# A hybrid decoder trunk: normed input of three token chunks from x given with tokens as columns, instead of transpositions by TensorE

## The chip, the cores and the metric

The kernel runs on one core of one Trainium2 chip. Its time is the device time of one execution in microseconds (us), the median of several runs. TensorE multiplies and transposes (PE in the profile; its weight loads are PEld), VectorE (DVE) and GpSimd (POOL) do elementwise work, ScalarE (ACT) elementwise work and the copies out of PSUM; SyncE (SP) and ACT issue the transfers. Each engine takes its instructions in the order in which the program issued them.

## The reference

Sequence 2048, model width 1024, one layer, float32:

```python
h = x * rsqrt(mean(x * x, axis=-1) + EPS) * norm_g          # _rmsnorm
proj = h @ w_in + b_in                                      # 1024 -> 4096
ua, za, ub, zb, ga, gb = split(proj)                        # 512 512 512 512 1024 1024
ya = s5_branch(ua, ...) * silu(za)      # diagonal complex state-space layer, gelu, glu
yb = pool_branch(ub, ...) * silu(zb)    # means over windows of 2, 4, 8, 16 tokens
merged = sigmoid(ga) * (ya @ w_branch_a) + sigmoid(gb) * (yb @ w_branch_b)
return _rmsnorm(x + merged @ w_out, final_norm_g)
```

## The kernel before

All products are done in pairs of float32r: an operand is split into a high part, rounded on ACT, and a low part, the difference, taken on DVE or POOL; `mm3` then issues three matmuls (high by high, high by low, low by high) for each slice of 128 of the contraction. The result has output channels on the partitions and tokens along the free axis, so the normed input must be there with model channels on the partitions: the tile `hT[c]` holds it for token chunk c (four chunks of 512 tokens), as 8 slices k of 128 channels, high and low. A block (c, n) is one tile of 128 output channels by 512 tokens: 8 slices, 24 matmuls of 128x512.

The first stage does the four blocks n = 0 to 3 of `ua` for each chunk in turn, (0,0), (0,1), ... (3,3), and makes `hT` meanwhile, one chunk ahead. After a block ACT evicts it (`uo`) and issues its store (`Ud`). Chunk c + 1 is made so: four tiles `xt` of 128 tokens are loaded; `mean_square` sums their squares, and `rsqrt` makes the roots with ten operations of four columns on DVE; `norm_tiles` multiplies each tile by its roots, on ACT and DVE for chunk 1 and on POOL for chunks 2 and 3; after blocks (c, 2) and (c, 3) `transpose_tile` transposes four slices each on TensorE, 16 transpositions into PSUM (`psT`), and splits them on the way out, with the gain of the norm as scale (high on ACT, low on DVE). The blocks of the stages behind (`za`, then `ub`, `zb`, `ga`, `gb`, scan, branches, output) follow on TensorE without a pause that is planned.

Names of weights: `wt` are split weights for later blocks, `w_first` those of the first stage (n = 1 to 3), `raw` their two staging buffers; `pump` loads the next raw block and splits the one that is there, so a load waits on SP until a staging buffer is free. `Later` (`pv`) holds the small operations that make the state-space parameters (tiles of 128x32) and issues so many behind each block on DVE. `WARM` is 17 transpositions of the identity (`psw`) that run before there is data.

Of the kernel before, what the change touches and what calls it, by code (L numbers as in the profile page):

```python
# [21 lines left out]
T = 8  # L22
# [14 lines left out]
def hybrid_kernel(ctx: ExitStack, tc: tile.TileContext, x, norm_g, w_in, b_in, log_dt, lam_re, lam_im,  # L37
                  b_re, b_im, c_re, c_im, ssm_d, w_glu, b_glu, pool_w, pool_scale, w_a, w_b, w_out,
                  final_g, out):
# [129 lines left out]
    def w_in_job(n, target):  # L169
        def load(raw):  # L170
            SP.dma_start(out=raw.rearrange("p (k n) -> p k n", k=NK),
                         in_=w_in[0][:, n * 128:(n + 1) * 128].rearrange("(k p) n -> p k n", p=128))
        add_job(("in", n), load, target)

    def branch_job(c, n):
        def load(raw):
            r = raw.rearrange("p (b k n) -> p b k n", b=2, k=NB)
            for b, w in enumerate((w_a, w_b)):
                SP.dma_start(out=r[:, b], in_=w[0][:, n * 128:(n + 1) * 128].rearrange("(k p) n -> p k n", p=128))
        add_job(("br", c, n), load, plain)  # L180
# [120 lines left out]
    def load_params(d):  # L301
        ldt = d.tile([128, G], F32, name="ldt")
        SP.dma_start(out=ldt, in_=log_dt[0].partition_broadcast(128))
        lam = d1.tile([G, 2, 128], F32, name="lam")
        for i, src in enumerate((lam_re, lam_im)):
            for h in range(2):
                SP.dma_start(out=lam[:, i, h * 64:(h + 1) * 64], in_=src[0])
        dn = d1.tile([G, C], F32, name="dn")
        SP.dma_start(out=dn, in_=ssm_d[0].rearrange("(g c) -> g c", c=C))
        return ldt, lam, dn  # L310

    def params(d, V, ldt, lam, dn):
# [16 lines left out]
        psl = mstile("psl")  # L329
        for i in range(2):  # L330
            PE.transpose(psl[:, i * G:(i + 1) * G], lam[:, i, :], idn[0:G, 0:G])
        PE.transpose(psl[0:C, 2 * G:3 * G], dn, idn[0:G, 0:G])
        lr, li = small("lr"), small("li")
        V.tensor_copy(out=lr, in_=psl[:, 0:G])
        V.tensor_copy(out=li, in_=psl[:, G:2 * G])
        V.tensor_copy(out=dc, in_=psl[0:C, 2 * G:3 * G])
# [191 lines left out]
    xts = {}  # L528

    def load_x(c):  # L530

        for i in range(4):
            tt = 4 * c + i
            if c in (1, 2):
                xt = xp.tile([128, D], F32, tag="xt", bufs=8, name="xt")
            else:
                xt = d1.tile([128, D], F32, tag="xt", bufs=4, name="xt")
            k0 = (tt % 2) * 128
            SP.dma_start(out=xt, in_=xr[tt // 2, k0:k0 + 128, :])
            xts[tt] = xt  # L540

    def mean_square(c):

        ss = d1.tile([128, 4], F32, tag="ss", bufs=2, name="ss")
        v = d1.tile([128, 4], F32, tag="v", bufs=2, name="v")
        for i in range(4):
            if c == 1 and i > 1:
                V.scalar_tensor_tensor(out=hT[c][:, 1, i - 1:i + 1, :].rearrange("p k n -> p (k n)"),
                                       in0=xts[4 * c + i], scalar=1.0, in1=xts[4 * c + i], op0=ALU.mult,
                                       op1=ALU.mult, accum_out=ss[:, i:i + 1])  # L550
            else:
                k = 2 * i if c == 3 else 0
                A.activation(hT[c][:, 0, k:k + 2, :].rearrange("p k n -> p (k n)"), xts[4 * c + i], AF.Square,
                             accum_out=ss[:, i:i + 1])
        V.tensor_scalar(out=v, in0=ss, scalar1=1.0 / D, scalar2=EPS, op0=ALU.mult, op1=ALU.add)
        return rsqrt(d1, v, 4)

    def norm_tiles(c):
        rstd = mean_square(c)
        for i in range(4):  # L560
            xt = xts[4 * c + i]
            if c > 1:
                GP.tensor_tensor(out=xt, in0=xt, in1=rstd[:, i:i + 1].broadcast_to([128, D]), op=ALU.mult)
# [11 lines left out]
    def first_block():  # L575

        rstd = mean_square(0)
# [10 lines left out]
        load_x(2)  # L588
# [27 lines left out]
    rows = d1.tile([48, 128], F32, name="rows")  # L616
    A.dma_start(out=rows[0:32, :], in_=b_in[0].rearrange("(n p) -> n p", p=128))
    A.dma_start(out=rows[32:40, :], in_=norm_g[0].rearrange("(n p) -> n p", p=128))
    A.dma_start(out=rows[40:44, :], in_=b_glu[0].rearrange("(n p) -> n p", p=128))
    A.dma_start(out=rows[44:48, :], in_=pool_scale[0].rearrange("(n p) -> n p", p=128))  # L620
    make_identity(nc, idn)
    psr = mstile("psr")
    PE.transpose(psr[:, 0:48], rows, idn[0:48, 0:48])
    V.tensor_copy(out=cols, in_=psr[:, 0:48])
    V.tensor_scalar(out=half, in0=psr[:, 0:48], scalar1=0.5, scalar2=0.0, op0=ALU.mult, op1=ALU.add)
# [12 lines left out]
    load_x(1)  # L638
    pv = Later(V)
    for c in range(NCH):  # L640
        for n in range(NB):
# [25 lines left out]
            pv.issue(26 if c + 1 == NCH else 10 if n > 1 else 20)  # L667
# [502 lines left out]
    for c in range(NCH):  # L1170
# [83 lines left out]
```

## Time and profile before

| | before |
|---|---|
| time, median of 3 runs (lowest, highest) | 1194.56 us (1194.1, 1196.18) |
| the profiled execution's own time | 1194.22 us |
| its span, first to last instruction | 1192.4 us |
| mean granted TensorE clock | 0.998 of full speed |
| PE, DVE, ACT, POOL busy | 98%, 60%, 33%, 27% of the span |

Times in the views count from the start of the span. The 1.8 us between the span and the time lie around it. Matmuls overlap in the pipeline: one is shown with some 0.39 us, but the next starts 0.23 us later, so distances between starts are to be read. A granted clock of 1.00 is 2.4 GHz, 0.50 is 1.2 GHz.

### The profile page before, as it was taken

Reading aid. Unit: us, or ns where it says so; the run is one execution under the profiler, and the core shown is the slowest. Engines: PE = TensorE matmul, PEld = TensorE weight load, DVE = VectorE, ACT = ScalarE, POOL = GpSimd, SP = SyncE. Lnnn points to the kernel's source line nnn. Section 1 sums busy time; section 2 is a strip of 40 time slices with the busy share of each in tenths; the row PEclk is TensorE's granted clock in tenths of the full one; section 3 lists DMA queues with packets and bytes.
Section 4 is the critical chain, followed back from the end, with each engine's and each line's share of the span. In section 5 each row is a group of like instructions: output and inputs, shape, how many; then the busy total and the mean of one; then the engine's idle time right before and its main releaser. Section 6 shows DMA issues by size and latency. Waiting matters only on the chain. (4 is left out here: it accounts for less than half of the span.)

```text
span 1192.4 us, 14803 instructions
## 1 busy us (share of the span) xinstructions
PE 1172.4 (98%) x5413; PEld 971.4 (81%) x5413; DVE 709.9 (60%) x1320; ACT 396.5 (33%) x622; POOL 325.0 (27%) x223
## 2 busy tenths in 40 slices
PE   6999999999999999999999999999999999999997
PEld 5887877888888888888888888888878888888886
DVE  4588399164344664887778873047665755755614
ACT  6542222122222232444334442244333332323202
POOL 2321077011012122432234321234223313213313
PEclk9999999999999999999999999999999999999999
DMA  8412334202111332433334332287875563563602
GB/s 293 151 43 82 67 116 139 75 18 73 36 38 56 98 96 90 132 110 108 106 102 128 100 105 81 70 265 247 273 227 197 177 198 138 176 211 115 198 7 88
DMA packets 149783, 149.94 MB, mean 126 GB/s; under 512 B 23584, under 2 KB 111184, under 8 KB 149712
## 3 DMA queue, kind: packets, MB, share of 16 engines
q1 hardware_dynamic: 127568, 112.54, 31.1%
q10 hardware_dynamic: 22144, 36.47, 8.2%
q8 instruction: 42, 0.69, 0.2%
q14 instruction: 29, 0.24, 0.1%
HBM read 99.43 MB, written 49.55 MB: 125 GB/s over the span
## 5 line engine op out<-in xcount | busy, mean ns | idle before, releaser
L104 PE MATMUL mm<-hT,wt 128*128 128x512 f32 x960 | 375.6, 391 | 0.0
L105 PE MATMUL mm<-hT,wt 128*128 128x512 f32 x960 | 374.4, 390 | 0.7 <-DVE hT L100 0.7
L106 PE MATMUL mm<-hT,wt 128*128 128x512 f32 x960 | 374.0, 390 | 0.1
L105 PEld LDWEIGHTS mm<-hT,wt 128*128 128x128 f32 x960 | 180.3, 188 | 38.3 <-DVE hT L100 1.9
L106 PEld LDWEIGHTS mm<-hT,wt 128*128 128x128 f32 x960 | 180.2, 188 | 38.3 <-DVE wt L148 0.4
L104 PEld LDWEIGHTS mm<-hT,wt 128*128 128x128 f32 x960 | 180.3, 188 | 36.7
L98 POOL TENSOR_TENSOR wt<-raw,wt 128x1024 fp32r<-128x1024 f32 x29 | 83.3, 2874 | 321.6 <-ACT wt L96 321.6
L1046 ACT ACTIVATE go<-mm,half 128x512 f32<-128x512 f32 x64 | 44.0, 688 | 189.6 <-PE mm L106 184.5
L104 PE MATMUL mm<-yab,wt 128*128 128x512 f32 x256 | 99.8, 390 | 1.2 <-DVE gt L1186 1.1
L106 PE MATMUL mm<-yab,wt 128*128 128x512 f32 x256 | 99.6, 389 | 0.0
L105 PE MATMUL mm<-yab,wt 128*128 128x512 f32 x256 | 99.6, 389 | 0.0
L1188 POOL TENSOR_TENSOR m<-gt 128x512 f32<-128x512 f32 x32 | 51.5, 1611 | 136.2 <-DVE gt L1186 102.8
L96 ACT ACTIVATE wt<-raw 128x1024 fp32r<-128x1024 f32 x61 | 64.5, 1057 | 68.5 <-PE mm L106 41.6
L1143 POOL TENSOR_TENSOR xt<-r,gb 128x512 f32<-128x512 f32 (+1 forms) x33 | 41.0, 1258 | 126.3 <-DVE r L1141 123.9
L98 DVE TENSOR_TENSOR wt<-raw,wt 128x1024 fp32r<-128x1024 f32 x32 | 59.9, 1873 | 18.9 <-ACT wt L96 18.9
L857 ACT ACTIVATE st<-mm,half 128x512 f32<-128x512 f32 x32 | 22.0, 688 | 131.2 <-PE mm L106 98.5
L1186 DVE SCALAR_TENSOR_TENSOR gt<-gt,mm 128x512 f32<-128x512 f32 x64 | 42.8, 681 | 36.8 <-PE mm L106 32.1
L104 PEld LDWEIGHTS mm<-yab,wt 128*128 128x128 f32 x256 | 48.1, 188 | 11.9 <-issue 1.9
L106 PEld LDWEIGHTS mm<-yab,wt 128*128 128x128 f32 x256 | 48.0, 188 | 10.0
L105 PEld LDWEIGHTS mm<-yab,wt 128*128 128x128 f32 x256 | 48.1, 188 | 9.8
L105 PE MATMUL mm<-wo,mt 128*128 128x512 f32 (+1 forms) x136 | 51.2, 377 | 0.0
L104 PE MATMUL mm<-wo,mt 128*128 128x512 f32 (+1 forms) x136 | 51.2, 377 | 0.0
(274 smaller groups left out, 1872.2 us busy)
## 6 DMA issues: line engine op xcount, KB each, us to landing
xt<-in_x SPq DMA_DIRECT2D x32, 512.0 KB, 5.5
raw<-in_w_in SPq DMA_DIRECT2D x32, 512.0 KB, 4.3
Gd<-go ACTq DMA_DIRECT2D x64, 256.0 KB, 2.2
gt<-Gd SPq DMA_DIRECT2D x32, 512.0 KB, 4.9
raw<-in_w_branch_a SPq DMA_DIRECT2D x32, 256.0 KB, 2.8
raw<-in_w_branch_b SPq DMA_DIRECT2D x32, 256.0 KB, 3.2
out<-xt ACTq DMA_DIRECT2D x31, 256.0 KB, 2.3
Ud<-uo ACTq DMA_DIRECT2D x16, 256.0 KB, 2.5
```

The source lines that it names most:

```text
L96: A.activation(hi, src, AF.Copy, scale=1.0 if scale is None else scale)
L98: (eng or V).tensor_tensor(out=lo, in0=src, in1=hi.bitcast(F32), op=ALU.subtract)
L104: PE.matmul(ps, lhsT=sh, rhs=mh, start=first, stop=False)
L105: PE.matmul(ps, lhsT=sh, rhs=ml, start=False, stop=False)
L106: PE.matmul(ps, lhsT=sl, rhs=mh, start=False, stop=last)
L857: A.activation(t, ps, AF.Tanh, bias=hcol(n), scale=0.5)
L1046: A.activation(o, ps, AF.Tanh, bias=hcol(n), scale=0.5)
L1143: GP.tensor_tensor(out=xt, in0=r, in1=gb[:, cs], op=ALU.mult)
L1186: V.scalar_tensor_tensor(out=gt[:, b], in0=gt[:, b], scalar=1.0, in1=pss[b], op0=ALU.add, op1=ALU.mult)
L1188: GP.tensor_tensor(out=m, in0=gt[:, 0], in1=gt[:, 1], op=ALU.add)
```

## The change

Chunk 0 stays as it was. For chunks 1 to 3:

- A second copy of x, `x_t`, with tokens as columns, is given beside x (laid out on the host). `load_xT` loads four tiles `xT` of 128x2x512 per chunk, which have model channels on the partitions already.
- The rows of x are loaded once more, into two buffers `xrow`, for the sums of squares alone, all on ACT (`squares`, in two pairs); the roots are made as before (`root`).
- `norm_row` makes the row of roots: four matmuls with the roots, broadcast, as stationary operand and the identity as moving one give a tile `psR` in which each partition holds the roots of the 512 tokens; ACT copies it to `R`.
- `norm_tile` multiplies a slice by its gain and by `R` in one DVE operation in place, then splits it from SBUF: high on ACT, low on DVE.
- The 96 transpositions of these chunks, the multiplications by roots on ACT, DVE and POOL, and the squares on DVE are gone.
- Vectors and matrices that were transposed on the chip at the start (`rows`, `lam`, `dn`) come laid out; the blocks of `w_in`, `w_branch_a`, `w_branch_b` and `w_glu` come each in one piece, so that a partition's row is one run of 4 KB where it was eight of 512 B.
- The small operations of `Later` go 12 behind each block where it was 20 or 10 (26 in chunk 3 as before).

The diff, cut to what the text speaks of:

```diff
--- before.py
+++ after.py
...
     def w_in_job(n, target):
         def load(raw):
-            SP.dma_start(out=raw.rearrange("p (k n) -> p k n", k=NK),
-                         in_=w_in[0][:, n * 128:(n + 1) * 128].rearrange("(k p) n -> p k n", p=128))
+            SP.dma_start(out=raw, in_=w_in[n])
         add_job(("in", n), load, target)
...
     def load_params(d):
         ldt = d.tile([128, G], F32, name="ldt")
         SP.dma_start(out=ldt, in_=log_dt[0].partition_broadcast(128))
-        lam = d1.tile([G, 2, 128], F32, name="lam")
-        for i, src in enumerate((lam_re, lam_im)):
-            for h in range(2):
-                SP.dma_start(out=lam[:, i, h * 64:(h + 1) * 64], in_=src[0])
-        dn = d1.tile([G, C], F32, name="dn")
-        SP.dma_start(out=dn, in_=ssm_d[0].rearrange("(g c) -> g c", c=C))
-        return ldt, lam, dn
-
-    def params(d, V, ldt, lam, dn):
+        lr, li = (d.tile([128, G], F32, name=n) for n in ("lr", "li"))
+        SP.dma_start(out=lr, in_=lam_re)
+        SP.dma_start(out=li, in_=lam_im)
+        SP.dma_start(out=dc, in_=ssm_d)
+        return ldt, lr, li
+
+    def params(d, V, ldt, lr, li):
...
-        psl = mstile("psl")
-        for i in range(2):
-            PE.transpose(psl[:, i * G:(i + 1) * G], lam[:, i, :], idn[0:G, 0:G])
-        PE.transpose(psl[0:C, 2 * G:3 * G], dn, idn[0:G, 0:G])
-        lr, li = small("lr"), small("li")
-        V.tensor_copy(out=lr, in_=psl[:, 0:G])
-        V.tensor_copy(out=li, in_=psl[:, G:2 * G])
-        V.tensor_copy(out=dc, in_=psl[0:C, 2 * G:3 * G])
...
-    xts = {}
+    xts, xrows, roots = {}, {}, {}

     def load_x(c):

         for i in range(4):
+            xts[i] = xt = d1.tile([128, D], F32, tag="xt", bufs=4, name="xt")
+            k0 = (i % 2) * 128
+            SP.dma_start(out=xt, in_=xr[i // 2, k0:k0 + 128, :])
+
+    def load_xT(c):
+
+        for h in range(4):
+            if c in (1, 2):
+                t = xp.tile([128, 2, 512], F32, tag="xt", bufs=8, name="xT")
+            else:
+                t = d1.tile([128, 2, 512], F32, tag="xt", bufs=4, name="xT")
+            SP.dma_start(out=t, in_=x_t[256 * h:256 * h + 256, 512 * c:512 * c + 512].rearrange("(k p) n -> p k n", p=128))
+            xts[c, h] = t
+
+    def load_rows(c, tiles):
+
+        for i in tiles:
             tt = 4 * c + i
-            if c in (1, 2):
-                xt = xp.tile([128, D], F32, tag="xt", bufs=8, name="xt")
-            else:
-                xt = d1.tile([128, D], F32, tag="xt", bufs=4, name="xt")
             k0 = (tt % 2) * 128
-            SP.dma_start(out=xt, in_=xr[tt // 2, k0:k0 + 128, :])
-            xts[tt] = xt
-
-    def mean_square(c):
-
-        ss = d1.tile([128, 4], F32, tag="ss", bufs=2, name="ss")
+            xrows[c, i] = t = d1.tile([128, D], F32, tag="xrow", bufs=2, name="xrow")
+            SP.dma_start(out=t, in_=xr[tt // 2, k0:k0 + 128, :])
+
+    def root(c, ss):
         v = d1.tile([128, 4], F32, tag="v", bufs=2, name="v")
-        for i in range(4):
-            if c == 1 and i > 1:
-                V.scalar_tensor_tensor(out=hT[c][:, 1, i - 1:i + 1, :].rearrange("p k n -> p (k n)"),
-                                       in0=xts[4 * c + i], scalar=1.0, in1=xts[4 * c + i], op0=ALU.mult,
-                                       op1=ALU.mult, accum_out=ss[:, i:i + 1])
-            else:
-                k = 2 * i if c == 3 else 0
-                A.activation(hT[c][:, 0, k:k + 2, :].rearrange("p k n -> p (k n)"), xts[4 * c + i], AF.Square,
-                             accum_out=ss[:, i:i + 1])
         V.tensor_scalar(out=v, in0=ss, scalar1=1.0 / D, scalar2=EPS, op0=ALU.mult, op1=ALU.add)
         return rsqrt(d1, v, 4)

-    def norm_tiles(c):
-        rstd = mean_square(c)
+    sums1 = {}
+
+    def squares(c, tiles):
+        if c not in sums1:
+            sums1[c] = d1.tile([128, 4], F32, tag="ss", bufs=2, name="ss")
+        for i in tiles:
+            t = xrows.pop((c, i))
+            A.activation(t, t, AF.Square, accum_out=sums1[c][:, i:i + 1])
+        if 3 in tiles:
+            roots[c] = root(c, sums1.pop(c))
+
+    def norm_row(c):
+
+        rstd = roots[c]
+        ps = mstile("psR")
         for i in range(4):
-            xt = xts[4 * c + i]
-            if c > 1:
-                GP.tensor_tensor(out=xt, in0=xt, in1=rstd[:, i:i + 1].broadcast_to([128, D]), op=ALU.mult)
-            elif i % 2:
-                A.activation(xt, xt, AF.Copy, scale=rstd[:, i:i + 1])
-            else:
-                V.tensor_scalar(out=xt, in0=xt, scalar1=rstd[:, i:i + 1], scalar2=None, op0=ALU.mult)
+            PE.matmul(ps[:, i * 128:(i + 1) * 128], lhsT=rstd[:, i:i + 1].broadcast_to([128, 128]), rhs=idn,
+                      start=True, stop=True)
+        roots[c] = t = d1.tile([128, 512], F32, tag="R", bufs=1, name="R")
+        A.activation(t, ps, AF.Copy)
+
+    def norm_tile(c, k):
+        t = xts[c, k // 2][:, k % 2]
+        V.scalar_tensor_tensor(out=t, in0=t, scalar=gcol(k), in1=roots[c], op0=ALU.mult, op1=ALU.mult)
+        split(t, hT[c][:, 0, k, :], hT[c][:, 1, k, :])

...
-        load_x(2)
...
-    rows = d1.tile([48, 128], F32, name="rows")
-    A.dma_start(out=rows[0:32, :], in_=b_in[0].rearrange("(n p) -> n p", p=128))
-    A.dma_start(out=rows[32:40, :], in_=norm_g[0].rearrange("(n p) -> n p", p=128))
-    A.dma_start(out=rows[40:44, :], in_=b_glu[0].rearrange("(n p) -> n p", p=128))
-    A.dma_start(out=rows[44:48, :], in_=pool_scale[0].rearrange("(n p) -> n p", p=128))
+    A.dma_start(out=cols, in_=vecs)
     make_identity(nc, idn)
-    psr = mstile("psr")
-    PE.transpose(psr[:, 0:48], rows, idn[0:48, 0:48])
-    V.tensor_copy(out=cols, in_=psr[:, 0:48])
-    V.tensor_scalar(out=half, in0=psr[:, 0:48], scalar1=0.5, scalar2=0.0, op0=ALU.mult, op1=ALU.add)
+    V.tensor_scalar(out=half, in0=cols, scalar1=0.5, scalar2=0.0, op0=ALU.mult, op1=ALU.add)
...
-    load_x(1)
+    load_rows(1, (0, 1))
+    load_xT(1)
     pv = Later(V)
     for c in range(NCH):
         for n in range(NB):
...
                 pump()
             if c == 0 and n == 0:
                 small = load_params(par)
-                load_x(3)
             o = stg.tile([128, 512], F32, tag="stg", name="uo")
             A.activation(o, ps, AF.Identity, bias=bcol(UA + n))
             A.dma_start(out=Ud[n][2 * c:2 * c + 2].rearrange("j g c k -> (g c) j k"),
                          in_=o.rearrange("p (j k) -> p j k", j=2))
+            if (c, n) == (0, 0):
+                squares(1, (0, 1))
+                load_rows(1, (2, 3))
+                load_xT(2)
+            elif (c, n) == (0, 1):
+                squares(1, (2, 3))
+                load_rows(2, (0, 1))
             if c + 1 < NCH:
-                if n == 0 and c == 0:
-                    norm_tiles(1)
-                if n >= 2:
-                    for k in range(4 * n - 8, 4 * n - 4):
-                        transpose_tile(c + 1, k)
-                    if (c, n) == (1, 3):
-                        s_x.close()
-                        open_hT(3)
-                if n == 3 and c + 2 < NCH:
-                    norm_tiles(c + 2)
+                if n == (0 if c else 2):
+                    norm_row(c + 1)
+                for k in (range(4 * n - 8, 4 * n - 4) if c == 0 else (2 * n, 2 * n + 1)):
+                    if k >= 0:
+                        norm_tile(c + 1, k)
+                if (c, n) == (1, 3):
+                    s_x.close()
+                    open_hT(3)
+                if c + 2 < NCH:
+                    if n == 2:
+                        squares(c + 2, (0, 1))
+                        load_rows(c + 2, (2, 3))
+                    elif n == 3:
+                        squares(c + 2, (2, 3))
+                        if c == 0:
+                            load_rows(3, (0, 1))
+                            load_xT(3)
             if c == NCH - 1 and n < 2:
                 pump()
             if (c, n) == (1, 0):
                 params(par, pv, *small)
-            pv.issue(26 if c + 1 == NCH else 10 if n > 1 else 20)
+            pv.issue(26 if c + 1 == NCH else 12)
...
+def lay_out(inputs):
...
+    r["x_t"] = r["x"][0].reshape(K, T, D).transpose(2, 1, 0).reshape(D, L)
...
+    r["w_in"] = blocks(r["w_in"][0], 128)
...```

Where the change moves instructions, three places show it. On ACT, from the store of block (0,2) (`Ud_82`) to that of (0,3) (`Ud_83`) and on to (1,0); `hT_178` is the normed input of chunk 1, `hT_182` of chunk 2. Before:

```order
L650 DMA Ud_82<-uo 128x2x256
L96 ACTIVATE hT_178<-psT,cols 128x512 x4
L649 ACTIVATE uo<-mm,cols 128x512
L650 DMA Ud_83<-uo 128x2x256
L96 ACTIVATE hT_178<-psT,cols 128x512 x4
L553 ACTIVATE hT_182,ss<-xt 128x1024 x4
L649 ACTIVATE uo<-mm,cols 128x512
```

Now:

```order
L649 DMA Ud_82<-uo 128x2x256
L566 ACTIVATE R<-psR 128x512
L95 ACTIVATE hT_178<-xT 128x512 x4
L554 ACTIVATE xrow,ss<-xrow 128x1024 x2
L648 ACTIVATE uo<-mm,cols 128x512
L649 DMA Ud_83<-uo 128x2x256
L95 ACTIVATE hT_178<-xT 128x512 x4
L554 ACTIVATE xrow,ss<-xrow 128x1024 x2
L648 ACTIVATE uo<-mm,cols 128x512
```

The copy of `R` stands ahead of the first four slices, and a pair of squares of chunk 2 stands between the first four slices and the eviction of (0,3), where all four squares stood behind the eight slices.

On DVE, the same stretch: behind the roots of chunk 1. Before, the roots (their last operation is the first row), two multiplications of chunk 1 and its eight low parts:

```order
L122 SCALAR_TENSOR_TENSOR rsy<-rsq,rsy 128x4
L567 TENSOR_SCALAR xt<-xt,rsy 128x1024 x2
L100 SCALAR_TENSOR_TENSOR hT_178<-psT,cols,hT_178 128x512 x8
L555 TENSOR_SCALAR v<-ss 128x4
```

Now (the first two of the eight slices are shown; six more such pairs follow):

```order
L121 SCALAR_TENSOR_TENSOR rsy<-rsq,rsy 128x4
L570 SCALAR_TENSOR_TENSOR xT<-xT,cols,R 128x512
L97 TENSOR_TENSOR hT_178<-xT,hT_178 128x512
L570 SCALAR_TENSOR_TENSOR xT<-xT,cols,R 128x512
L97 TENSOR_TENSOR hT_178<-xT,hT_178 128x512
L570 SCALAR_TENSOR_TENSOR xT<-xT,cols,R 128x512
```

Each slice has two DVE operations where it had one, and the low part of a slice (which waits for ACT's high part) stands ahead of the next slice's multiplication.

On SP, the loads of the first 35 us. Before:

```order
L539 DMA xt<-in_x 128x1024 x4
L171 DMA raw<-in_w_in 128x8x128 x2
L539 DMA xt<-in_x 128x1024 x8
L171 DMA raw<-in_w_in 128x8x128 x3
L303 DMA ldt<-in_ssm_log_dt 128x32
L307 DMA lam<-in_ssm_lam_re 32x64 x2
L307 DMA lam<-in_ssm_lam_im 32x64 x2
L309 DMA dn<-in_ssm_d 32x16
L539 DMA xt<-in_x 128x1024 x4
```

Now:

```order
L522 DMA xt<-in_x 128x1024 x4
L170 DMA raw<-in_w_in 128x1024 x2
L540 DMA xrow<-in_x 128x1024 x2
L531 DMA xT<-in_x_t 128x2x512 x4
L170 DMA raw<-in_w_in 128x1024 x3
L300 DMA ldt<-in_ssm_log_dt 128x32
L302 DMA lr<-in_ssm_lam_re 128x32
L303 DMA li<-in_ssm_lam_im 128x32
L304 DMA dc<-in_ssm_d 16x32
L540 DMA xrow<-in_x 128x1024 x2
```

The second pair of rows of chunk 1 (last row) stands behind three weight blocks and four small loads; before, all rows of chunks 1 and 2 were requested ahead of these.

## Rows read from the trace of the kernel before

**Rows 1.** The page, part 1: busy us (share of the span), instructions of each engine.

```profile
PE 1172.4 (98%) x5413; PEld 971.4 (81%) x5413; DVE 709.9 (60%) x1320; ACT 396.5 (33%) x622; POOL 325.0 (27%) x223
```

**Rows 2.** Timeline of PE, first stage: start, duration, engine, line, instruction [idle before <- releaser].

```profile
34.98 1.91 PE L572 MATMUL psT<-idn,xt 128*128 128x128 f32 x16
36.65 0.48 PE L104 MATMUL mm<-hT,w_first 128*128 128x512 f32 x1
...
95.63 2.63 PE L572 MATMUL psT<-idn,xt 128*128 128x128 f32 x16 [1.10 <-DVE hT L100]
98.02 0.48 PE L104 MATMUL mm<-hT,wt 128*128 128x512 f32 x1
...
120.19 0.39 PE L104 MATMUL mm<-hT,wt 128*128 128x512 f32 x1
```

**Rows 3.** Groups of the whole run: busy us, mean ns | idle before, releaser.

```profile
L100 DVE SCALAR_TENSOR_TENSOR yhl<-yraw,yhl 128x512 fp32r<-128x512 f32 x16 | 10.2, 686 | 42.9 <-ACT yhl L96 42.9
...
L98 DVE TENSOR_TENSOR bt<-mr,bt 128x512 fp32r<-128x512 f32 x8 | 5.5, 692 | 6.4 <-ACT bt L96 6.4
...
L96 ACT ACTIVATE bt<-mr 128x512 fp32r<-128x512 f32 x8 | 5.1, 632 | 9.4 <-DVE spl L98 9.0 <-ACT go L1046 0.4
...
L649 ACT ACTIVATE uo<-mm,cols 128x512 f32<-128x512 f32 x16 | 11.0, 685 | 47.6 <-PE mm L106 47.6
```

**Rows 4.** Timeline of POOL, low parts of two weight blocks.

```profile
21.25 2.40 POOL L98 TENSOR_TENSOR wt<-raw,wt 128x1024 fp32r<-128x1024 f32 x1 [18.81 <-ACT wt L96]
25.14 3.13 POOL L98 TENSOR_TENSOR w_first<-raw,w_first 128x1024 fp32r<-128x1024 f32 x1 [1.50 <-ACT w_first L96]
```

**Rows 5.** Timeline of ACT and its queue (ACTq: the issue of a transfer).

```profile
24.00 1.06 ACT L96 ACTIVATE w_first<-raw 128x1024 fp32r<-128x1024 f32 x1 [1.52 <-DMA raw<-in_w_in]
...
25.67 0.41 ACTq L650 DMA_DIRECT2D Ud<-uo  x1
26.13 1.06 ACT L553 ACTIVATE hT<-xt 128x1024 fp32r<-128x1024 f32 x1 [0.49 <-ACT uo L649]
...
27.31 1.06 ACT L553 ACTIVATE hT<-xt 128x1024 fp32r<-128x1024 f32 x1
```

**Rows 6.** Timeline of SP's queue: start and duration of the issues.

```profile
28.72 0.58 SPq L303 DMA_DIRECT2D ldt<-in_ssm_log_dt  x1
...
31.72 1.96 SPq L539 DMA_DIRECT2D xt<-in_x  x4
```

**Rows 7.** The tile xt, four issues from 0 to 3 us, and four from 31 to 34 us.

```profile
DMA to landing us min/median/max: 3.9/5.1/6.4
```

```profile
DMA to landing us min/median/max: 5.5/6.4/7.2
```

**Rows 8.** Timeline of DVE, the ten operations of the roots of chunk 1, first and last.

```profile
28.49 0.17 DVE L555 TENSOR_SCALAR v<-ss 128x4 f32<-128x4 f32 x1 [2.49 <-ACT hT L553]
...
30.29 0.17 DVE L122 SCALAR_TENSOR_TENSOR rsy<-rsq,rsy 128x4 f32<-128x4 f32 x1
```

**Rows 9.** Groups of DVE from 60.3 to 67.2 us: small operations of the parameters.

```profile
L298 DVE TENSOR_SCALAR t<-t 128x32 f32<-128x32 f32 x15 | 2.6, 180 | 0.4
```

**Rows 10.** Timeline of PE at the start: the warm-up and the first transpositions of data.

```profile
7.56 3.66 PE L635 MATMUL psw<-idn 128*128 128x128 f32 x17
...
12.28 2.05 PE L572 MATMUL psT<-idn,xt 128*128 128x128 f32 x12 [1.05 <-DMA xt<-in_x]
```

**Rows 11.** Timeline of PE, the longest wait of the stage of the branches.

```profile
873.31 0.47 PE L104 MATMUL mm<-yab,wt 128*128 128x512 f32 x1 [1.13 <-DVE gt L1186]
```

**Rows 12.** Windows after the last matmul: stretch, PE, PEld, DVE, ACT, POOL busy, granted clock, DMA, GB/s.

```profile
1184.00:1186.00 2.00, 0.00 (x0) 0.00 (x0) 0.95 (x4) 1.18 (x3) 0.72 (x1) 1.00 0.33 125
1188.00:1189.00 1.00, 0.00 (x0) 0.00 (x0) 0.37 (x1) 0.60 (x1) 0.00 (x0) 0.73 0.00 0
1189.00:1190.00 1.00, 0.00 (x0) 0.00 (x0) 0.00 (x0) 0.00 (x0) 0.00 (x0) 0.50 0.76 283
```

More of the change, by code (lines that the diff above doesn't have):

```diff
@@ L36, in hybrid_kernel @@
 @with_exitstack
-def hybrid_kernel(ctx: ExitStack, tc: tile.TileContext, x, norm_g, w_in, b_in, log_dt, lam_re, lam_im,
-                  b_re, b_im, c_re, c_im, ssm_d, w_glu, b_glu, pool_w, pool_scale, w_a, w_b, w_out,
-                  final_g, out):
+def hybrid_kernel(ctx: ExitStack, tc: tile.TileContext, x, x_t, vecs, w_in, log_dt, lam_re, lam_im,
+                  b_re, b_im, c_re, c_im, ssm_d, w_glu, pool_w, w_a, w_b, w_out, final_g, out):
     nc = tc.nc
@@ L176, in load @@
         def load(raw):
-            r = raw.rearrange("p (b k n) -> p b k n", b=2, k=NB)
             for b, w in enumerate((w_a, w_b)):
-                SP.dma_start(out=r[:, b], in_=w[0][:, n * 128:(n + 1) * 128].rearrange("(k p) n -> p k n", p=128))
+                SP.dma_start(out=raw[:, b * 512:(b + 1) * 512], in_=w[n])
         add_job(("br", c, n), load, plain)
@@ L575, in first_block @@
     def first_block():
-        rstd = mean_square(0)
+        ss = d1.tile([128, 4], F32, tag="ss", bufs=2, name="ss")
+        for i in range(4):
+            A.activation(hT[0][:, 0, 0:2, :].rearrange("p k n -> p (k n)"), xts[i], AF.Square, accum_out=ss[:, i:i + 1])
+        rstd = root(0, ss)
         rest = pump(V)
@@ L957, in load @@
         def load(raw):
-            SP.dma_start(out=raw.rearrange("p (k n) -> p k n", k=NB),
-                         in_=w_glu[0][:, h * 256:(h + 1) * 256].rearrange("(k p) n -> p k n", p=128))
+            SP.dma_start(out=raw, in_=w_glu[h])
         def target(key):
@@ L1229, in hybrid_kernel, with blocks @@
     s_r.close()
-_INS = ["x", "norm_g", "w_in", "b_in", "ssm_log_dt", "ssm_lam_re", "ssm_lam_im", "ssm_b_re", "ssm_b_im",
-        "ssm_c_re", "ssm_c_im", "ssm_d", "ssm_w_glu", "ssm_b_glu", "pool_w", "pool_scale", "w_branch_a",
-        "w_branch_b", "w_out", "final_norm_g"]
+_INS = ["x", "x_t", "vecs", "w_in", "ssm_log_dt", "ssm_lam_re", "ssm_lam_im", "ssm_b_re", "ssm_b_im",
+        "ssm_c_re", "ssm_c_im", "ssm_d", "ssm_w_glu", "pool_w", "w_branch_a", "w_branch_b", "w_out", "final_norm_g"]
+def lay_out(inputs):
+    import numpy as np
+    r = {name: np.asarray(a) for name, a in inputs.items()}
+    def blocks(w, n):
+        k = w.shape[0] // 128
+        return w.reshape(k, 128, w.shape[1] // n, n).transpose(2, 1, 0, 3).reshape(-1, 128, k * n)
+    r["x_t"] = r["x"][0].reshape(K, T, D).transpose(2, 1, 0).reshape(D, L)
+    r["vecs"] = np.concatenate([r[name][0].reshape(-1, 128) for name in
+                                ("b_in", "norm_g", "ssm_b_glu", "pool_scale")]).T
+    r["w_in"] = blocks(r["w_in"][0], 128)
+    r["w_branch_a"] = blocks(r["w_branch_a"][0], 128)
+    r["w_branch_b"] = blocks(r["w_branch_b"][0], 128)
+    r["ssm_w_glu"] = blocks(r["ssm_w_glu"][0], 256)
+    for name in ("ssm_lam_re", "ssm_lam_im"):
+        r[name] = np.concatenate([r[name][0].T] * 2)
+    r["ssm_d"] = r["ssm_d"][0].reshape(G, C).T
+    return r
 def kernel(**inputs):
@@ L1242 @@
     nc = bacc.Bacc("TRN2", target_bir_lowering=False, num_devices=1)
+    inputs = lay_out(inputs)
     arrays, args = {}, []
```

## The prediction

> **What bounds the kernel now.** First the page's busy times: PE works 98% of the span, all others 60% or less [rows 1]. So a microsecond counts only where PE waits or does work that can go, and a pause of PE in the first stage moves the end by as much, since what follows runs without slack. Then the timeline of PE through the first stage. Block (0,2) ends at 34.98, the stage at 120.19 [rows 2]: 85.2 us for 13 blocks. The last four take 98.02 to 120.19, 5.54 each; 13 of them are 72.1. The other 13.1 us are the six groups of 16 transpositions (1.67 us where nothing is late, 34.98 to 36.65) and their waits: the last group starts late behind DVE's low parts and costs 2.4. This 13.1 is what the change can take away, and what new waits are to be set against.
>
> **What a slice of normed input costs.** Before, 16 transpositions gave four slices, and ACT and DVE split them behind the matmuls. Now a slice is a chain: DVE multiplies, ACT takes the high part, DVE the low part, and in DVE's order the low part stands ahead of the next slice's multiplication. Nothing of the next slice on DVE can lie under ACT's part. The nearest forms from SBUF take 0.686 (two tensors and a scalar), 0.632 (ACT's high part) and 0.692 (difference) [rows 3]: 2.01 per slice, and I take 2.0, with 1.9 to 2.15 as ends (a few hundredths of overlap at the hand-overs, or a tenth of latency). A block uses a slice in 5.54 / 8 = 0.69. So eight slices take 16 us in which PE does under three blocks, and where they are begun late, PE waits.
>
> **W1, the roots of chunk 1.** `norm_row(1)` stands on PE behind (0,2), and its roots need all four squares. The second pair of rows is requested on SP behind three weight blocks, the last of which waits until POOL frees a staging buffer. POOL ends the first block at 23.65 and the second needs 2.4 to 3.1 [rows 4]. Before, that one began only at 25.14, behind a raw block that landed late: ACT waited for it until 24.00 [rows 5]. With runs of 4 KB I let it land in time, so the buffer is free at 26.1 to 26.8; if it lands as late as before, at 28.3. One weight request and four small ones at 0.5 (six in 28.72 to 31.72 [rows 6]) put the rows' request at 28.5 to 29.2. A first row tile lands 3.9 to 5.5 later [rows 7], the second some 1.3 behind it (landing grows by 2.5 over three tiles that were issued 0.45 apart). One square is 1.2 (26.13 to 27.31 [rows 5]), the roots 2.0 (28.49 to 30.46 [rows 8]). Together 36.9 to 39.2, against 34.98: W1 is 1.9 to 4.2, middle 3.0, and 5.7 with the late block. The four matmuls of `psR` add 0.5, from 16 in 1.67 and a fill. (0,3) runs from 38.5 to 44.1.
>
> **W2, chunk 1 in time for (1,0).** `R` is there at 39.3 (38.5, a copy of 0.63, a hand-over). Slices 0 to 3 take until 47.3. Then ACT has work in between: a pair of squares, 2.3 from start to DVE [rows 5, 8], the eviction of (0,3), 0.69 [rows 3], and its request, 0.46 (25.67 to 26.13 [rows 5]). Slice 3's high part ended at 46.6, so slice 4's begins at 50.1; its low part ends at 51.4, that of slice 7 at 57.4. The last three matmuls of (1,0) need that one, and the block ends 0.7 later, at 58.1, where it would have ended at 49.6: W2 is 8.5.
>
> **W3.** `norm_row(2)` stands on PE behind (1,0); its roots stand behind the last pair of squares, behind the last high part (56.7): 56.7 + 2.3 + 2.0 = 61.0, so 2.9, and 0.5 for `psR`. Blocks (1,1) to (1,3) then end at 78.2.
>
> **W4 to W6.** Chunk 2: `R` at 62.3, eight slices 16.0, and between the four pairs three times twelve small operations, 0.18 with 0.03 between them [rows 9]: 7.6. The last slice is there at 85.9, (2,0) ends at 86.6 where it would have at 83.7: W4 is 2.9. Roots of chunk 3, as W3: W5 is 2.9 and 0.5. Chunk 3, the same chain: W6 is 2.9. (3,0) ends at 115.1 and the stage at 131.8.
>
> Waits and `psR` are 24.6 together in place of 13.1, so the stage ends **11.6 later** (131.8 against 120.2). All of POOL's multiplications, ACT's and DVE's for the roots that go were off PE's path: nothing for them but what the chains above hold.
>
> **The other edits.** The warm-up waited for the little loads of vectors and ran from 7.56 for 3.66 us, up to the first data at 12.28 [rows 10]. Now it can run at once, and PE is idle for several microseconds ahead of the data. After the last matmul the clock still read 1.00 two microseconds on, and 0.73 and then 0.50 after 4 us without a matmul [rows 12]; so the first block may begin at 1.2 GHz. What the slow warm-up cost bounds it: 17 transpositions in 3.66 against 1.8 at the rate of 16 in 1.67, so 0 to 1.9; I take 0.7. The weight blocks in longer runs can shorten waits for weights later: the longest of the stage of the branches is 1.1, behind DVE, itself late behind weights [rows 11]; I take 0.5 off, 0 to 1.1. Other blocks' loads lie under matmuls: nothing. If that cover goes, in W1, it is counted there. The small operations sum to as many as before, and chunk 3 still takes the rest: nothing beyond W4 and W6.
>
> Sum against the profiled execution: 1194.2 + 11.6 + 0.7 - 0.5 = 1206.0; it lies 0.3 below the median, so the forecast is **1206**.
>
> **The rivals.**
> The forecast (0.67). Its ends: W1 -1.1 and +1.2 (+2.7 with the late block); a slice of 1.9 or 2.15 moves W2, W4 and W6 (24 slices) by -2.4 or +3.6; the clock -0.7 or +1.2; the branches +0.5 or -0.6. Most of them do not fall together: 1202 to 1210.
>
> The clock falls in the new waits (0.14). In W1 and W3 PE stands idle for 3 us, and in W2 it does 0.69 of work every 2.0. The rows after the last matmul show 1.00 for the first two idle microseconds and the fall after four; so W3, ahead of which PE worked only a third of the time, is the place. Against it: no wait is as long as that idle stretch. A fall costs what the warm-up lost, 1.9, and two or three of them 4 to 6 less what lies under the slices: 1209 to 1211. The Trainium skill ("TensorE: Matmul & The Clock Gate", section "Loop structure matters more than you think") says that a long wait between matmuls makes TensorE go cold, and that a loop should keep them back to back while other engines work. By that rule the time is this rival's, some 1210; the trace agrees with it as far as the tail, 0.50 at 1189.
>
> The other side: slices cost DVE's own time alone (0.08). If ACT's part lay under DVE's, a slice were 1.38; then W2 is 0.9 (ACT's squares and eviction fill the gap), W4 and W6 are nothing, W5 is 0.3, the waits and `psR` sum to 9 in place of 13.1, and the time is 1190 (1186 to 1193). It decides from some 1.5 per slice down. For it: the two DVE forms alone sum to that. Against it: the order on DVE, and the idle time of those groups, which the profile puts down to ACT's high parts almost wholly (42.9 of 42.9 [rows 3]).
>
> No change (0.05): half of this, a slice of some 1.6 with W1 near 2, 1192 to 1197. And a load that comes later than any row above (0.06): rows of chunk 2 or 3, each behind squares that free its buffer, over 1212.
>
> **How the numbers follow.** 0.2% (2.4 us) is about what a measurement can tell here. Faster takes the other side, 0.08; same 0.05; slower the rest, 0.87. The range runs from 1200, two below the forecast's own low end for a shorter W2, to 1212, which takes in the clock's case; below lie 0.13, above 0.06.
>
> **What the profile will show.** PE's timeline: `psR` of chunk 1 starting near 38 behind DVE's roots; in (1,0) three matmuls every 2 us, released by DVE's low parts; `za` beginning near 132. DVE's low parts waiting for ACT's high parts, eight times 0.6 for each chunk. The granted clock 1.00 through 35 to 135. Wrong would be: slices at 1.5 or less, `psR` of chunk 1 behind (0,2) without a wait, or a clock of 0.5 between blocks; also a later stage that gains or loses more than 2 us.

## The result and the profile after

The changed kernel takes 1211.59 us (median of 4 runs, 1210.3 to 1214.43), the kernel before 1194.8 beside it; the ratio is 1.0142 (1.0124 to 1.016). It is slower by 16.8 us, where 11.8 were forecast; the time lies inside the range, at its upper end. The profiled execution took 1210.3 us with a span of 1208.5.

The page of the changed kernel, parts 1 and 2 (busy times; granted clock in 40 slices):

```profile
PE 1176.4 (97%) x5337; PEld 970.1 (80%) x5337; DVE 706.7 (58%) x1334; ACT 398.2 (33%) x627; POOL 307.8 (25%) x215
...
PEclk8888999999999999999999999999999999999999
```

All engines do about as much as before [rows 1]; only the first four slices (30 us each) show a lower clock. The loss is in the first stage, and PE's timeline there answers to [rows 2] (cuts marked by dots):

```profile
38.87 1.13 PE L563 MATMUL psR<-idn,rsy 128*128 128x128 f32 x8 [3.69 <-DVE rsy L121]
39.75 0.66 PE L103 MATMUL mm<-hT,w_first 128*128 128x512 f32 x1
...
46.97 0.39 PE L103 MATMUL mm<-hT,wt 128*128 128x512 f32 x1
...
49.49 0.39 PE L105 MATMUL mm<-hT,wt 128*128 128x512 f32 x1
52.34 0.51 PE L103 MATMUL mm<-hT,wt 128*128 128x512 f32 x1 [2.46 <-ACT hT L95]
...
59.81 0.63 PE L105 MATMUL mm<-hT,wt 128*128 128x512 f32 x1
62.64 2.05 PE L563 MATMUL psR<-idn,rsy 128*128 128x128 f32 x8 [2.21 <-DVE rsy L121]
64.34 0.77 PE L103 MATMUL mm<-hT,wt 128*128 128x512 f32 x1
...
82.45 0.39 PE L103 MATMUL mm<-hT,wt 128*128 128x512 f32 x1
...
89.66 0.39 PE L105 MATMUL mm<-hT,wt 128*128 128x512 f32 x1
92.96 2.05 PE L563 MATMUL psR<-idn,rsy 128*128 128x128 f32 x8 [2.91 <-DVE t L295]
94.66 0.77 PE L103 MATMUL mm<-hT,wt 128*128 128x512 f32 x1
...
112.95 0.39 PE L103 MATMUL mm<-hT,wt 128*128 128x512 f32 x1
...
119.40 0.50 PE L104 MATMUL mm<-hT,wt 128*128 128x512 f32 x1 [0.22 <-DVE hT L97]
...
136.65 0.39 PE L103 MATMUL mm<-hT,wt 128*128 128x512 f32 x1
```

W1 is the first line (38.87 against an end of (0,2) at 35.02), W2 the block that begins at 46.97 and whose last matmul starts at 59.81, W3 the wait to 62.64, then W4 (in the block from 82.45 to 89.66), W5 (to 92.96) and W6 (in the block that begins at 112.95). The stage ends at 136.65, against 120.19: 16.5 later. From there to the end of the span are 1071.85 us, before 1072.21: the rest of the program is 0.4 shorter.

DVE in the same stretch, slices 0, 1 and 4 of chunk 1:

```profile
42.11 0.69 DVE L97 TENSOR_TENSOR hT<-xT,hT 128x512 fp32r<-128x512 f32 x1 [0.69 <-ACT hT L95]
42.72 0.75 DVE L570 SCALAR_TENSOR_TENSOR xT<-xT,cols,R 128x512 f32<-128x512 f32 x1
44.16 0.69 DVE L97 TENSOR_TENSOR hT<-xT,hT 128x512 fp32r<-128x512 f32 x1 [0.70 <-ACT hT L95]
...
48.88 0.74 DVE L570 SCALAR_TENSOR_TENSOR xT<-xT,cols,R 128x512 f32<-128x512 f32 x1
52.31 0.69 DVE L97 TENSOR_TENSOR hT<-xT,hT 128x512 fp32r<-128x512 f32 x1 [2.69 <-ACT hT L95]
```

From low part to low part are 2.05 us, of which DVE waits 0.70 for ACT. Ahead of slice 4 it waits 2.69: ACT does a pair of squares and an eviction first. The windows over W2, W3 and block (1,1) (stretch, PE, PEld, DVE, ACT, POOL busy, granted clock, DMA, GB/s) show what the forecast held for less likely:

```profile
45.00:50.00 5.00, 4.88 (x22) 3.63 (x20) 3.22 (x5) 3.03 (x5) 0.00 (x0) 1.00 0.03 13
50.00:55.00 5.00, 1.96 (x4) 0.77 (x4) 1.99 (x4) 2.15 (x5) 0.00 (x0) 0.85 0.78 255
55.00:60.00 5.00, 4.79 (x9) 2.08 (x8) 2.77 (x5) 2.83 (x5) 0.00 (x0) 0.50 0.03 9
60.00:64.00 4.00, 1.79 (x8) 1.39 (x7) 1.64 (x10) 1.16 (x3) 0.00 (x0) 0.50 0.87 262
64.00:70.00 6.00, 6.00 (x23) 4.90 (x22) 3.19 (x7) 1.86 (x3) 0.00 (x0) 0.73 0.92 333
```

In W2 the clock goes from 1.00 (2.4 GHz) to 0.50 (1.2 GHz). `psR` of chunk 2 takes 1.70 (62.64 to 64.34), and (1,1) takes 6.9 (64.34 to 71.25) in place of 5.54. So: is the loss the chain of slices, the clock, or both?

### The profile page after: what moved, and what is told of

The parts are those of the page before. It is cut to its first block, busy times and chain, and to the rows that moved or that the text cites. A ratio compares the mean times of both kernels' runs of the same rounds, so it can differ in the third digit from the quotient of the medians.

```text
span 1208.5 us, 14670 instructions
## 1 busy us (share of the span) xinstructions
PE 1176.4 (97%) x5337; PEld 970.1 (80%) x5337; DVE 706.7 (58%) x1334; ACT 398.2 (33%) x627; POOL 307.8 (25%) x215
## 5 line engine op out<-in xcount | busy, mean ns | idle before, releaser
L103 PE MATMUL mm<-hT,wt 128*128 128x512 f32 x960 | 378.7, 395 | 4.3 <-ACT hT L95 4.1
L104 PE MATMUL mm<-hT,wt 128*128 128x512 f32 x960 | 377.4, 393 | 1.2 <-DVE hT L97 0.9
L105 PE MATMUL mm<-hT,wt 128*128 128x512 f32 x960 | 375.8, 391 | 0.0
L103 PEld LDWEIGHTS mm<-hT,wt 128*128 128x128 f32 x960 | 181.6, 189 | 44.5 <-ACT hT L95 7.8
L104 PEld LDWEIGHTS mm<-hT,wt 128*128 128x128 f32 x960 | 181.5, 189 | 41.6 <-DVE hT L97 3.8
L105 PEld LDWEIGHTS mm<-hT,wt 128*128 128x128 f32 x960 | 181.4, 189 | 37.9 <-DVE wt L147 0.3
L97 POOL TENSOR_TENSOR wt<-raw,wt 128x1024 fp32r<-128x1024 f32 x29 | 83.1, 2867 | 391.2 <-ACT wt L95 391.2
L103 PE MATMUL mm<-yab,wt 128*128 128x512 f32 x256 | 99.6, 389 | 0.0
L105 PE MATMUL mm<-yab,wt 128*128 128x512 f32 x256 | 99.6, 389 | 0.0
L104 PE MATMUL mm<-yab,wt 128*128 128x512 f32 x256 | 99.6, 389 | 0.0
L95 ACT ACTIVATE wt<-raw 128x1024 fp32r<-128x1024 f32 x61 | 64.5, 1057 | 64.0 <-PE mm L105 39.6
L97 DVE TENSOR_TENSOR wt<-raw,wt 128x1024 fp32r<-128x1024 f32 x32 | 60.5, 1890 | 16.9 <-ACT wt L95 16.9
L103 PEld LDWEIGHTS mm<-yab,wt 128*128 128x128 f32 x256 | 48.0, 188 | 10.1
L104 PEld LDWEIGHTS mm<-yab,wt 128*128 128x128 f32 x256 | 48.0, 188 | 10.0
L105 PEld LDWEIGHTS mm<-yab,wt 128*128 128x128 f32 x256 | 48.0, 188 | 9.9
L104 PE MATMUL mm<-wo,mt 128*128 128x512 f32 (+1 forms) x136 | 51.2, 377 | 0.0
L103 PE MATMUL mm<-wo,mt 128*128 128x512 f32 (+1 forms) x136 | 51.2, 377 | 0.0
```

What stands on the lines that cost most here:

```text
L95: A.activation(hi, src, AF.Copy, scale=1.0 if scale is None else scale)
L97: (eng or V).tensor_tensor(out=lo, in0=src, in1=hi.bitcast(F32), op=ALU.subtract)
L103: PE.matmul(ps, lhsT=sh, rhs=mh, start=first, stop=False)
L104: PE.matmul(ps, lhsT=sh, rhs=ml, start=False, stop=False)
L105: PE.matmul(ps, lhsT=sl, rhs=mh, start=False, stop=last)
```

## The experiments

The kernel before took 1195.89 us beside the first filled run, the order, the rows and the layout; 1195.58 beside the second filled run, order and rows together, and the version with everything earlier; 1195.84 beside the last two. Ratios are to the kernel before beside each run, with a 95% interval.

**Transpositions of the identity in the waits.** They need no data and feed nothing; they are there to keep the clock up. 64 more stand at the start.

```diff
-WARM = 17
+WARM = 81
...
         rstd = roots[c]
+        fill({1: 32, 2: 20, 3: 24}[c])
         ps = mstile("psR")
...
         for k in range(NK):
+            if (c, n) == (1, UA) and k > 2:
+                fill(16 if k == 4 else 8)
```

> The changed kernel with transpositions of the identity put where TensorE waits: 64 more at the start, 32, 20 and 24 ahead of the three psR, and 8 to 16 ahead of slices 3 to 7 of block (1,0). They need no data and fit into the waits. Theory: the time beyond the forecast is the clock, which falls in these waits, so that psR and the first third of the blocks (0,3), (1,1), (2,1) run at 1.2 GHz. Then the granted clock stays at 1.00 through 140 us, those blocks take 5.6 in place of 6.9 to 7.2, each psR under 0.9 in place of up to 1.7, and the time is 1205 to 1206.5. Rival: these blocks are slow for another reason (late slices, late weights) and the clock only shows it: then the blocks stay at 6.9 or more and the time is 1211 or, with transpositions that don't fit, more.

1209.91 us, 1.0113 (1.0098 to 1.0128): between the two, and its interval overlaps that of the changed kernel. PE's timeline of this kernel at the second `psR`, and its windows over (1,0), over the second `psR`, and over (3,0) and the start of (3,1):

```profile
62.60 1.13 PE L569 MATMUL psR<-idn,rsy 128*128 128x128 f32 x8 [0.52 <-DVE rsy L121]
63.48 0.47 PE L103 MATMUL mm<-hT,wt 128*128 128x512 f32 x1
```

```profile
50.00:55.00 5.00, 4.10 (x29) 3.10 (x26) 2.03 (x4) 2.42 (x5) 0.00 (x0) 1.00 0.78 255
55.00:60.00 5.00, 4.52 (x27) 3.48 (x28) 2.72 (x5) 2.88 (x5) 0.00 (x0) 1.00 0.02 7
60.00:64.00 4.00, 3.48 (x30) 3.22 (x28) 1.65 (x10) 1.27 (x4) 0.00 (x0) 1.00 0.79 239
...
114.00:119.00 5.00, 3.38 (x7) 1.93 (x8) 3.37 (x12) 1.43 (x3) 0.00 (x0) 0.75 0.00 0
119.00:124.00 5.00, 5.00 (x14) 3.90 (x13) 4.59 (x15) 1.58 (x2) 2.40 (x1) 0.56 0.16 56
```

Up to (3,0) the clock stays at 1.00, `psR` takes 0.88 and (1,1) 5.6. And yet the second `psR` begins at 62.60, where it began at 62.64: the roots set it, not PE. PE reached the next chunks sooner and waited longer for their slices; in (3,0) the waits were then longer, the clock fell there, and (3,1), behind which no slice is waited for, took 7.7. The stage ended at 137.5, no sooner than without the fill (136.65).

**The same, with (2,0) and (3,0) filled too.**

```diff
+            if (c, n) in ((2, UA), (3, UA)) and k > 5:
+                fill(8)
```

> The kernel with transpositions of the identity in the waits, and eight more ahead of slices 6 and 7 in the blocks (2,0) and (3,0), where the clock still fell (115 to 123 us) in the first run of this kind. Theory: the stage is paced by the chain of slices on DVE and ACT, so a slow block that has a wait ahead of the next chunk costs nothing, and only slow psR (0.85 each) and a slow (3,1), behind which no slices are waited for, cost time; then (3,1) takes 5.5 in place of 7.7, the stage ends at 135 to 136 and the time is 1207 to 1208.5. Rival: the clock's loss adds up wherever it falls: then this kernel, with a clock of 1.00 throughout, is 5 to 6 below the changed kernel, 1206 or less.

1207.51 us, 1.0101 (1.0086 to 1.0116). The clock is 1.00 in every window of the stage, which ends at 135.06. The time lies where the first theory put it, but its interval begins at 1205.9, so the time alone does not exclude the rival. The trace speaks against the rival: (0,3) takes 1.5 less than in the changed kernel, and yet the second `psR` starts 23.5 behind the first, there 23.8. A part of the expectation fails all the same: (3,1) takes 5.5 in the changed kernel too (119.97 to 125.45), so its gain is one over the first filled run alone.

**The order on DVE.** The low part of a slice is held back until the next slice is multiplied.

```diff
-        split(t, hT[c][:, 0, k, :], hT[c][:, 1, k, :])
+            A.activation(hT[c][:, 0, k, :], t, AF.Copy)
+            if late:
+                late()
+            late = lambda t=t, k=k: V.tensor_tensor(out=hT[c][:, 1, k, :], in0=t, in1=hT[c][:, 0, k, :].bitcast(F32),
+                                                    op=ALU.subtract)
```

> The changed kernel with one thing moved: on DVE the multiplication of the next slice stands ahead of the low part of this one, within a group of slices. Theory: a slice costs 2.05 because DVE stands still under ACT's part; now it costs DVE's own two operations, 1.4. Then W2 falls from 7.5 to 3.5, W4 (1.9) and W6 (1.4) go, W5 shrinks by 1 to 2, and the time is 1200 to 1203. Rival: the rate is set by ACT or by hand-overs between the engines, a slice stays near 2.0, and the time is 1210 to 1212.

1197.74 us, 1.0013 (1.0003 to 1.0024): 13.9 under the changed kernel (14.5 under its second measurement, below), more than expected. Its DVE timeline in chunk 1:

```profile
42.97 0.75 DVE L572 SCALAR_TENSOR_TENSOR xT<-xT,cols,R 128x512 f32<-128x512 f32 x1
43.63 0.69 DVE L576 TENSOR_TENSOR hT<-xT,hT 128x512 fp32r<-128x512 f32 x1
44.23 0.74 DVE L572 SCALAR_TENSOR_TENSOR xT<-xT,cols,R 128x512 f32<-128x512 f32 x1
...
46.28 1.41 DVE L572 SCALAR_TENSOR_TENSOR xT<-xT,cols,R 128x512 f32<-128x512 f32 x2
50.13 0.69 DVE L576 TENSOR_TENSOR hT<-xT,hT 128x512 fp32r<-128x512 f32 x1 [2.44 <-ACT hT L573]
```

A slice now costs 1.26 (42.97 to 44.23), without a wait. What stays are the squares on ACT ahead of slice 4 (2.44), W1, and the waits for roots. PE's third `psR` starts 1.7 behind the last matmul ahead of it, and the stage ends at 124.59, still 4.4 behind the kernel before.

**The rows of chunk 1 at the start.** Two of them go into buffers that the columns of chunk 2 take later; all squares stand behind (0,0).

```diff
-    load_rows(1, (0, 1))
+    load_rows(1, (0, 1, 2, 3))
...
-                squares(1, (0, 1))
-                load_rows(1, (2, 3))
+                squares(1, (0, 1, 2, 3))
                 load_xT(2)
             elif (c, n) == (0, 1):
-                squares(1, (2, 3))
```

> The changed kernel with all four row tiles of chunk 1 requested at the start, two of them into buffers that the columns of chunk 2 take later, and all four squares behind block (0,0). Theory: W1 (3.85) comes only from the second pair of rows, requested near 29; then psR of chunk 1 follows (0,2) without a wait, (0,3) runs at full clock (5.6 in place of 7.2), everything behind moves forward, and the time is 1205 to 1206.5. Without a part of the clock in it, 1207.5 to 1208. Rival: another thing is late then (the split of the next weight block behind four squares, or the columns), and W1 or W2 takes back what is won: 1210 to 1212.

1207.31 us, 1.0094 (1.0081 to 1.0108). `psR` follows (0,2) at 35.44 without a wait. The stage ends at 133.38, 3.3 sooner, as its first `psR` starts 3.4 sooner: about W1 alone. That (0,3) runs at full clock here, 1.5 quicker, brings nothing on top in this profile: the second `psR` starts 24.0 behind the first, in the changed kernel 23.8, since the slow run of (0,3) lay ahead of W2. The time can't tell the two parts of the theory apart; it lies between them, with an interval of 1.6 to either side.

**The layout of weights alone,** on the kernel before: contiguous blocks of `w_in`, `w_branch_a`, `w_branch_b`, `w_glu`, and nothing else.

```diff
-            SP.dma_start(out=raw.rearrange("p (k n) -> p k n", k=NK),
-                         in_=w_in[0][:, n * 128:(n + 1) * 128].rearrange("(k p) n -> p k n", p=128))
+            SP.dma_start(out=raw, in_=w_in[n])
```

> The kernel before with only the weight blocks of w_in, w_branch_a, w_branch_b and w_glu laid out in one piece. Theory: they lie under matmuls, and what is left is 0 to 1.1 off the stage of the branches: 1193.5 to 1194.8. Rival: waits for weights are worth more than that, here or through queues: 1192 or less; or the early loads come in another order and delay the rows of x: 1196 or more.

1194.75 us, 0.9988 (0.998 to 0.9997), 0.4 to 2.4 us less (the edit to `w_in` is shown, the others are alike); the wait of [rows 11] is gone from its trace. The expected size, and a small one.

**Order and rows together.**

> The reordered DVE operations and the early rows of chunk 1 together. Theory: W1 and the slices lie one behind the other on one chain, so both gains add: 13 of the order and 4 to 5 of the rows; psR of chunk 1 behind (0,2) without a wait, a slice 1.4, the time 1192 to 1194, a little below the kernel before. Rival: with quick slices the wait moves to the pair of squares and the eviction on ACT that stand between slices 3 and 4, so that half of the gain of the rows is lost: 1195 to 1197.

1194.27 us, 0.9991 (0.9981 to 1.0001). The time lies just above the theory's upper end, 3.5 below the order alone; it can't be told from the kernel before. `psR` of chunk 1 waits for nothing, but those of chunks 2 and 3 start 2.6 and 2.4 behind the last matmul ahead of them, where matmuls that wait for nothing follow at 0.23. The trace does not show the rival's loss: the three `psR` start 3.5, 3.2 and 3.4 sooner than with the order alone, so the gain of the rows is kept. Yet the stage ends only 1.9 sooner (122.73), for another reason: behind the longer wait for the third `psR` the clock falls, (2,1) takes 7.1 in place of 5.6, and nothing waits in the block behind it (3,0), which takes 5.5. The window over the first half of (2,1), columns as above:

```profile
82.00:86.00 4.00, 4.00 (x14) 3.26 (x14) 3.73 (x13) 1.86 (x3) 0.00 (x0) 0.57 0.00 0
```

With 1196.52 this execution is one of the longer of the eleven, from 1192.2 to 1196.76; the others have no trace.

**Everything that the slices wait for, a block earlier.**

```diff
+            if (c, n, k) == (0, UA + 2, 2):
+                norm_row(1)
+                norm_slices(1, (0, 1))
...
+                if n == 0:
+                    squares(c + 1, (2, 3))
...
+                elif n == 1:
+                    norm_row(c + 1)
+                    norm_slices(c + 1, (0, 1, 2))
```

> As the run before, and everything that the slices wait for is moved one block or more ahead: half of the squares of chunk 1 on DVE, psR of chunk 1 inside (0,2), its slices from there on, squares of chunks 2 and 3 behind the last slices of the chunk ahead, their psR behind (1,1) and (2,1), the small operations mostly behind n = 0. Theory: then no block waits, the stage costs its blocks and three psR of 0.9, the stage ends near 110 in place of 120 before, and the time is 1183 to 1187, some 10 under the kernel before. Rival: rows of x land late or ACT (two squares more in a row, evictions) holds the slices, and one or two waits of 3 to 5 with a slow clock behind them remain: 1189 to 1194.

1192.95 us, 0.9975 (0.9963 to 0.9986): the rival. PE's three waits are for roots. The second of them is shown; the profile names `t`, a small operation that starts at 57.65, right behind the last operation of the roots (57.57):

```profile
57.88 0.35 PE L571 MATMUL psR<-idn,rsy 128*128 128x128 f32 x1 [3.25 <-DVE t L295]
```

and ACT shows what the roots wait for, the last row tile of chunk 2, requested only at 48.2, when a buffer came free, and landed some 6 later:

```profile
54.59 1.06 ACT L562 ACTIVATE xrow<-xrow 128x1024 f32<-128x1024 f32 x1 [2.74 <-DMA xrow<-in_x]
```

**The changed kernel again, and rows in buffers of their own.** The last version gives the rows of chunks 2 and 3 buffers that chunks 0 and 1 have left, does half of the squares of chunk 2 on DVE, and puts `psR` inside (0,2), (1,1) and (2,1). It also moves squares of chunk 3, slices of chunk 3 and the small operations. The diff is against the run before, cut to buffers and `psR`:

```diff
-            if c == 1 and i > 1:
+            if c == 1 and i > 1 or c == 3:
                 t = xp.tile([128, D], F32, tag="xt", bufs=8, name="xrow")
+            elif c == 2:
+                t = d1.tile([128, D], F32, tag="xt", bufs=4, name="xrow")
...
+            if (c, n, k) == (1, UA + 1, 5):
+                norm_row(2)
+            if (c, n, k) == (2, UA + 1, 4):
+                norm_row(3)
```

> The changed kernel once more, in the same rounds as the next run: 1210 to 1213, so that the 3 to 5 us that the kernels with filled waits and with early rows gained stand against a value with more runs.

1212.2 us, 1.0135 (1.0118 to 1.0152).

> The earlier version with everything moved ahead still waits three times for roots (1.8, 3.6 and 2.9), because rows of chunks 2 and 3 land late, each behind squares that free its two buffers. Here the rows of chunk 2 go into the buffers that chunk 0 left, those of chunk 3 into those of chunk 1's columns, half of the squares of chunk 2 are on DVE, and psR stands inside (0,2), (1,1) and (2,1). Theory: what was left is the landing of rows; then no block of the stage waits more than 1, it ends near 111, ten below the kernel before, and the time is 1184 to 1187. Rival: the chain of slices itself (1.4 each with small operations between) reaches the next chunk's first block late, and 1189 to 1192 remains.

1183.66 us, 0.99 (0.9885 to 0.9914): a little below what was expected, and 12 under the kernel before. Its PE timeline at the second `psR` and at the end of the stage:

```profile
50.56 0.39 PE L105 MATMUL mm<-hT,wt 128*128 128x512 f32 x1
50.78 1.05 PE L573 MATMUL psR<-idn,rsy 128*128 128x128 f32 x8
51.59 0.48 PE L103 MATMUL mm<-hT,wt 128*128 128x512 f32 x1
...
110.09 0.39 PE L103 MATMUL mm<-hT,wt 128*128 128x512 f32 x1
```

No wait is left at the three `psR`, and `psR` costs 0.81. Which of the things that were moved at once brought this, the buffers or the rest, no run separates.

## Why the prediction was right, and where it was off

The direction, the places and the order of the waits were right: W1 to W6 all stand in the trace, with the releasers that were named but for one: of the three matmuls of a slice the first waits for ACT's high part, and only the second for DVE's low part. The likeliest case did not hold in full. Its own ends were 1202 and 1210, and two of its terms failed, the clock and the size of `psR`; the range held because its upper end took in the rival of the clock. It held with little to spare: two of the four runs, and the median of the second measurement (1212.2), lie above 1212. That part is luck.

- **A slice.** Forecast 2.0, measured 2.05, and the run with the other order shows the cause: without DVE standing still under ACT's part a slice is 1.26 to 1.27 and the kernel some 14 us quicker. The rival on the other side had the lever right, but not the price: for slices of 1.38 it said 1190, and with 1.26 the time is 1197.74, because W1, the waits for roots and a third of W2 stay. What kept it away was the order on DVE, as the idle time of such pairs [rows 3] had shown.
- **W1.** 3.85 where 3.0 was the middle: the second row tile landed 2.4 behind the first (squares at 33.23 and 35.59), not 1.3. In the second profile of the changed kernel W1 is 3.1, so it varies from run to run. The early weight block was right: its high part ran at 22.45, not 24.00 [rows 5] (23.05 with the layout alone), and POOL was done at 26.1.
- **W2 to W6.** Block (1,0) ended 2.1 later than forecast, of which W1 had brought 0.9, the first `psR` 0.4, the slices 0.4, and its last three matmuls at 1.2 GHz 0.4. Waits of roots behind the last slices (W3, W5) were 2.4 and 3.1 for 2.9. W2, W4 and W6 were 7.7, 1.9 and 1.5 for 8.5, 2.9 and 2.9: smaller, because a slow block lay ahead of each (see the clock, below).
- **`psR`.** Sized from transpositions, 0.5 each. Four such matmuls appear as eight records and take 0.88, and 1.70 at 1.2 GHz. That is 1.2 more for each of the two behind a slow block, half of the 4.85 by which the stage ended later than forecast (136.65 against 131.8).
- **The clock.** Here the likeliest case failed as a description: the forecast had 1.00 from 35 to 135, and its rival was what the trace shows, behind W1, in W2 and in W5, though no single wait was longer than W1. The rival's price, 3 to 5 above the forecast, is not refuted, but its parts are other ones than the 1.9 that it took for each fall. Blocks (0,3), (1,1) and (2,1) lost 1.4 to 1.6 each. For (0,3) the filled runs and the early rows show that this hardly counts: it lies ahead of a wait for slices of the next chunk. For the other two the smaller W4 and W6 say the same. With order and rows together, where no wait for slices follows (2,1), its 1.5 are lost in full. The slow `psR`, 0.8 each, do stand on the path. Holding the clock through the stage was worth 4 to 5 by the medians (1207.51 against 1211.59 and 1212.2), 1.6 and 3.2 by the ends of the stage in the profiles (135.06 against 136.65 and 138.24), which are single executions; between these the runs don't decide, and two slow `psR` explain 1.6 of it. The Trainium skill ("TensorE: Matmul & The Clock Gate", section "Loop structure matters more than you think") says that a long wait between matmuls makes TensorE cold; the trace agrees, 0.50 from 55 to 64. What it cost here depended on what was waited for next.
- **The start.** 0.7 was taken for a slow first block. The windows do show 0.50 from 10 to 15, but (0,2) ends at 35.02, as before at 34.98. The first block waits for DVE in both (until 18.39 here, 18.33 before), and that wait takes up the slow start. In the second profile (0,2) ends at 35.60, so 0 to 0.6 is what the two show.
- **Later stages.** -0.5 was taken, -0.4 measured, and 0.4 to 2.4 less for the layout alone.

The sum: 1194.2 + 16.5 - 0.4 = 1210.3, the profiled execution's time; the median lies 1.3 above it. The sign held because W1 to W6, counted with the slow blocks ahead of them, came to some 25 where 23 had been worked out. The missing 4.85 are 2.8 from `psR` (1.6 of it the clock), 0.9 from the landing of rows and some 1.2 from 24 slices at 2.05, not a wait that nobody had named.

## What to carry to other kernels

Work that is taken off the busiest engine must be counted again as a chain on the engines that take it over: here two operations on DVE with one on ACT between them, in an order that let nothing overlap, cost more than the 96 transpositions they replaced; with the other order alone the two came within 0.3% of each other. Ask for each new chain what it waits for first (roots, rows, buffers) and whether that can be a block earlier; the same computation with another order and other buffers went from 1% slower to 1% faster. A slow clock, like any lateness, was paid here in the main where no other wait followed.

## What was not expected of the hardware

- A matmul of 128x128 in float32 with a broadcast stationary operand is recorded twice here: 12 such matmuls give 24 records, where each transposition gives one; four take 0.81 at full clock, 16 transpositions 1.67 [rows 2].
- Without a wait between them, a multiplication and a difference on DVE that are shown with 0.75 and 0.69 follow each other at 0.66 and 0.60: a pair costs 1.26, less than the sum of the two.
